# Whole VectorE passes, three steps moved to ScalarE, and tiles moved within 128 bytes in a two-block transformer kernel

## The chip, the cores and the metric

The kernel runs on one core of one Trainium2 chip. The metric is the device time of one execution in microseconds, as the median of several runs. Engines are called as the profile calls them: PE (TensorE), DVE (VectorE), ACT (ScalarE), POOL (GpSimd), SP (SyncE, which issues the loads).

## The reference

Two blocks run one after the other on x, 256 tokens of 2048 features, in fp32. Each block draws six modulation vectors from a conditioning vector c, mixes tokens in two ways, and ends with an FFN that has a causal convolution of width 3:

```python
mod = silu(c) @ w_ada + b_ada            # 2048 x 12288: six vectors of 2048
shift_m, scale_m, gate_m, shift_f, scale_f, gate_f = split(mod, 6)
h = rms_norm(x) * (1 + scale_m) + shift_m
proj = h @ w_in
# block 1: attention (8 heads of 128, own block, rel. bias) and an SSM (16 heads of 64, one chunk of 256)
#   p = softmax(logits);  attn = p @ v
#   y = (C B^T * exp(segsum(A))) @ (x * dt)
# block 2: a RWKV-7 scan (16 heads of 64) and window means (pool)
mix = concat(mixer_a, mixer_b) @ w_out
x = x + gate_m * mix
h = rms_norm(x) * (1 + scale_f) + shift_f
u = causal_dwconv3(h @ w_up)             # 2048 -> 2 x 5632
x = x + gate_f * ((silu(g) * val) @ w_down)   # g, val: the halves of u
```

A final rms_norm closes each block. Nearly all of the work is the products with w_in, w_out, w_up and w_down.

## The kernel before

**Products.** Tokens lie along the free axis (T = 256), so each matmul has a 128x128 weight tile as the stationary operand and 256 columns of x as the moving one, summed in a PSUM bank `acc`. An fp32 product is made of three float32r matmuls: weights and inputs are each split into a high part and a remainder, and `blk` issues hi·xh, hi·xl and lo·xh. A column of outputs (16 k-tiles, one 1 MB load into a tile `raw`) is worked off in two halves of 8 k-tiles. For each half ACT writes the high part `whi` in two pieces of 512 columns (`hi_steps`), DVE writes the remainder `wlo` = raw − whi in two pieces of 512 columns (`lo_steps`), and PE runs 24 matmuls. `raw` and `whi` and `wlo` have four buffers each, and the splitting runs two halves ahead of PE. The next load is issued by SP when the last half's `wlo` has been written (`issue`).

**The inputs** of a product are tiles [128, 512] whose first 256 columns are the high part and whose last 256 the remainder: h (tiles named `area`), the mixers' outputs (`mixa`, `mixb` in block 1, `mixA`, `mixB` in block 2), and the FFN's gated values, one tile `g` [128, 16, 512]. Where each lies within 128 bytes follows from the order in which the pools are filled: `whi`, `wlo` and `raw` at 64, the tiles of h at 0 in both FFNs, `mixa` and `mixb` at 96, `mixA` at 64, `g` at 96 in block 1 and at 64 in block 2, the tile `cb` at 96.

**Modulation.** A row of w_ada is a 1 MB load, mostly into a `raw` or a `mixb` tile that is not needed yet, in the FFNs into two tiles of their own (`far`). `ada` multiplies it with c (spread over the partitions in `cb`) on DVE and sums along the row, in two passes of 1024 columns that end in one column each of `mod` and `half`; each is followed by a read of DVE's accumulator, and `after` adds `half` to `mod`. Block 2 draws its late vectors (`adk`) in another way that is not touched.

**Attention and SSM** run as generators beside the products (one head, or one pair of heads, at a time). In attention the tile `L` holds logits, then probabilities; DVE normalises them with two `tensor_scalar` (128 and 256 columns) by `nm`, and copies the head's output out of PSUM to `at`, which lies in `mixa`. In the SSM a pair of heads has a tile `sg` [128, 768] with the decays (exp on ACT), which DVE multiplies with `G` (C·B^T) and with dt (`dtk`) in four `scalar_tensor_tensor`; `X` is a copy of the inputs out of PSUM by ACT.

**The order** on each engine is settled when the program is recorded: a clock model with a cost for each operation (`poll`) decides after each matmul block which generator's next step is put on its engine's queue. Every engine then works off its own queue in order. All instructions are recorded by one helper, line 302, so the profile's groups are told apart by the names of the tiles.

**The stages**, in us of the span: the first 16 columns of w_in with 32 modulation rows (0 to 165); the rest of w_in with attention and SSM (165 to 385); w_out of block 1 (385 to 515); its FFN (to 1269), three chunks of 32, 32 and 24 up columns (48 matmuls each) that each end with 16 down columns (48, 48 and 36 matmuls): up to 703, 974 and 1201 with the down columns of the first two from 703 to 793 and 974 to 1066; then block 2: w_in with the scan (1270 to 1640), w_out (1680 to 1762), and its FFN (1762 to 2508), with down columns from 1950 to 2041, 2215 to 2306 and 2437 to 2505. Between the FFN's up and down columns there is no break in PE's work.

Of the kernel before, what the change touches and what calls it, by code (L numbers as in the profile page):

```python
# [355 lines left out]
class K:  # L356
# [111 lines left out]
    def extra_steps(self, i, e):  # L468
# [6 lines left out]
        if e[0] == 'ada':  # L475
            return [lambda j=j: self.ada(e, j) for j in range(2)]
# [64 lines left out]
    def ada(self, e, j=0):  # L541
# [249 lines left out]
    def setup(self, ctx):  # L791
# [22 lines left out]
        self.half1 = self.pb1.tile([128, 96], F32, name='half1')  # L814
        self.half2 = c.tile([128, 96], F32, name='half2')
# [180 lines left out]
    def ffn_entries(self, blk, last_hook):  # L996
# [18 lines left out]
        for c, nk in enumerate(CH):  # L1015
            for j in range(j0, j0 + nk):
# [9 lines left out]
                def d2(acc, cv=cv, cg=cg, k=j - j0):  # L1026
                    y = yield from conv(acc, cv)
                    g = self.fg['g']
# [4 lines left out]
                    self.act(g[:, k, 0:T], y, AF.Identity)  # L1033
                    yield 'V'
                    self.nc.vector.tensor_sub(g[:, k, T:2 * T], y, g[:, k, 0:T].bitcast(F32))
                out.append(('w', self.full(A[f'wup{blk}'][2 * j], self.hrhs, d1)))
                out.append(('w', self.full(A[f'wup{blk}'][2 * j + 1], self.hrhs, d2)))
            for n in range(16):
# [7 lines left out]
                out.append(('w', self.full(A[f'wdn{blk}_{c}'][n], lambda k: self.fg['g'][:, k], d, nk)))  # L1046
# [5 lines left out]
    def wout_entries(self, blk, order, last_hook):  # L1052
        mod = self.mod1 if blk == 1 else self.mod2
        out = []
        for q, half in enumerate(order):
            for pr in range(8):
                ds = []
                for n in (2 * pr, 2 * pr + 1):
                    def d(acc, n=n, q=q):
                        assert (blk, 2) in self.ada_done  # L1060
                        yield from self.resid(acc, n, mod[:, 32 + n:33 + n])
                        if q == 1:
# [4 lines left out]
                                               lambda k: self.mix[k], ds)))  # L1067
# [27 lines left out]
    def attn_gen(self, h, box):  # L1095
# [36 lines left out]
        nc.vector.tensor_scalar(L[:, 0:128], L[:, 0:128], nm[:, 2:3], None, op0=MUL)  # L1132
        nc.vector.tensor_scalar(L[:, 128:384], L[:, 128:384], nm[:, 3:4], None, op0=MUL)
# [139 lines left out]
    def ssm_gen(self, i):  # L1273
# [11 lines left out]
        self.act(X, ps[:, 0:256], AF.Copy)  # L1285
# [872 lines left out]
```

## Time and profile before

| | |
|---|---|
| median of 3 runs | 2517.81 us (2504.33 to 2522.46) |
| profiled execution | 2520.43 us, span 2518.7 us, mean granted clock 0.978 |
| busy share of the span | PE 95%, DVE 81%, ACT 51%, POOL 3% |
| moved | 617.08 MB, mean 245 GB/s |
| chain that ended last | PE 74%, DVE 20%, issue 3%, ACT 2%, DMA 1% |

The span is the time from the first to the last instruction of the profiled execution; 1.7 us of its time lie around it. It is 2.6 us above the median. The shares are means over stages with different limits, so the table only says where to look: PE is busy nearly everywhere, DVE is next.

### The profile page before, as it was taken

What the parts mean: (1) busy time and instruction counts of PE and PEld (TensorE: products, weight loads), DVE (VectorE), ACT (ScalarE), POOL (GpSimd) and SP (SyncE); (2) the same over time, 40 slices, a digit from 0 to 9 for tenths busy, and PEclk for the clock granted to TensorE, in tenths of its full rate; (3) what the DMA queues carried; (4) which work ended last, traced back from release to release, by engine and by line L of the source; (5) the groups of instructions that cost most, each with busy time, mean ns of one, the idle gap of its engine ahead of it and who ended that gap; (6) DMA issues with size and microseconds to landing.
All of it is one profiled execution on the core that took longest, in us unless ns stands there. A gap on an engine that the chain in (4) does not pass through costs nothing.

```text
span 2518.7 us, 54091 instructions
## 1 busy us (share of the span) xinstructions
PE 2396.3 (95%) x22262; PEld 2323.6 (92%) x22262; DVE 2048.9 (81%) x4023; ACT 1280.0 (51%) x2515; POOL 80.3 (3%) x190
## 2 busy tenths in 40 slices
PE   6789898899999999999999999999999999999998
PEld 5779887899999999999988888889899999999998
DVE  6889999989878988787777999988898566755765
ACT  3236544455544554455566554434655455544554
POOL 0000000000000000000001222100000000000000
PEclk9899999899999999999999999989999999999999
DMA  9988787858787888785563444568687555555553
GB/s 347 347 319 316 269 300 286 314 207 315 290 311 287 304 299 301 288 297 197 190 210 126 160 168 170 201 235 301 234 310 274 185 184 199 187 198 184 188 178 123
DMA packets 93321, 617.08 MB, mean 245 GB/s; under 512 B 10473, under 2 KB 13809, under 8 KB 25233
## 3 DMA queue, kind: packets, MB, share of 16 engines
q1 hardware_dynamic: 89794, 604.93, 65.8%
q0 software_dynamic: 1984, 7.35, 0.8%
q8 instruction: 174, 2.85, 0.4%
q10 hardware_dynamic: 1296, 1.35, 0.2%
q14 instruction: 73, 0.60, 0.1%
HBM read 609.39 MB, written 4.21 MB: 244 GB/s over the span
## 4 chain that ended last, share of the span: by engine, by line
PE 74%; DVE 20%; issue 3%; ACT 2%; DMA 1%; ACTq 0%; DVEq 0%; SPq 0%
PE acc L302 68%; DVE wlo L302 4%; PE sB L302 4%; DVE raw L302 4%; DVE area L302 2%; DVE mixb L302 2%; ACT whi L302 1%; DVE t L302 1%; DVE adk L302 1%; PE sA L302 1%; DVE sg L302 1%; DVE slo L302 1%; DMA far<-wada 1%; DVE CK L302 0%; ACT area L302 0%
## 5 line engine op out<-in xcount | busy, mean ns | idle before, releaser
L302 PE MATMUL acc<-area,whi 128*128 128x256 f32 x8128 | 1474.9, 285 | 43.1 <-ACT area L302 39.5
L302 PEld LDWEIGHTS acc<-area,whi 128*128 128x128 f32 x8128 | 1260.3, 191 | 63.3 <-ACT area L302 45.3
L302 PE MATMUL acc<-area,wlo 128*128 128x256 f32 x3968 | 1113.2, 281 | 22.1 <-DVE wlo L302 21.8
L302 ACT ACTIVATE whi<-raw 128x512 fp32r<-128x512 f32 (+1 forms) x1472 | 834.8, 613 | 402.5 <-PE acc L302 309.4
L302 DVE TENSOR_TENSOR wlo<-raw,whi 128x512 fp32r<-128x512 f32 (+1 forms) x1472 | 930.2, 674 | 86.6 <-ACT whi L302 85.0
L302 PEld LDWEIGHTS acc<-area,wlo 128*128 128x128 f32 x3968 | 753.9, 190 | 25.3 <-DVE wlo L302 25.3
L302 PE MATMUL acc<-g,whi 128*128 128x256 f32 x2816 | 499.7, 281 | 0.0
L302 PEld LDWEIGHTS acc<-g,whi 128*128 128x128 f32 x2816 | 431.4, 188 | 0.0
L302 PE MATMUL acc<-g,wlo 128*128 128x256 f32 x1408 | 395.3, 281 | 0.0
L302 DVE SCALAR_TENSOR_TENSOR fy<-acc,vec,fy 128x255 f32<-128x255 f32 x352 | 169.1, 481 | 145.9 <-ACT fy L302 139.5
L302 PEld LDWEIGHTS acc<-g,wlo 128*128 128x128 f32 x1408 | 265.0, 188 | 0.0
L302 ACT ACTIVATE fy<-acc,vec 128x256 f32<-128x256 f32 x176 | 99.2, 565 | 262.3 <-PE acc L302 262.3
L302 DVE SCALAR_TENSOR_TENSOR far<-far,cb 128x1024 f32<-128x1024 f32 x160 | 191.2, 1218 | 11.8 <-DMA far<-wada 11.8
L302 DVE SCALAR_TENSOR_TENSOR area<-acc,mod,area 128x256 f32<-128x256 f32 x160 | 77.0, 481 | 102.1 <-PE acc L302 102.0
L302 DVE SCALAR_TENSOR_TENSOR raw<-raw,cb 128x1024 f32<-128x1024 f32 (+1 forms) x81 | 118.3, 1494 | 0.1
L302 ACT ACTIVATE area<-t,mod 128x256 fp32r<-128x256 f32 x64 | 32.2, 507 | 125.8 <-DVE t L302 125.8
L302 DVE SCALAR_TENSOR_TENSOR adk<-raw,vec,adk 128x512 f32<-128x512 f32 x120 | 91.0, 758 | 2.4
L302 DVE SCALAR_TENSOR_TENSOR mixb<-mixb,cb 128x1024 f32<-128x1024 f32 (+1 forms) x47 | 67.9, 1464 | 4.2 <-DMA mixb<-wada 4.2
L302 ACT ACTIVATE g<-fy 128x256 fp32r<-128x256 f32 x88 | 36.6, 416 | 67.3 <-DVE fy L302 67.3
L302 ACT ACT_TABLE_LOAD x48 | 61.6, 1283 | 12.1 <-DVE area L302 4.7
L302 ACT ACTIVATE t<-area 128x256 f32<-128x256 f32 x90 | 35.5, 411 | 61.2 <-DVE area L302 58.9
L302 ACT ACTIVATE fs<-fy 128x256 f32<-128x256 f32 x88 | 36.7, 417 | 47.7 <-DVE fy L302 46.0
(262 smaller groups left out, 1992.6 us busy)
## 6 DMA issues: line engine op xcount, KB each, us to landing
raw<-wup SPq DMA_DIRECT2D x176, 1024.0 KB, 6.3
far<-wada SPq DMA_DIRECT2D x80, 1024.0 KB, 4.9
raw<-win SPq DMA_DIRECT2D x64, 1024.0 KB, 5.5
raw<-wdn SPq DMA_DIRECT2D x64, 1024.0 KB, 5.2
raw<-wada SPq DMA_DIRECT2D x51, 1024.0 KB, 6.9
raw<-wout SPq DMA_DIRECT2D x32, 1024.0 KB, 5.5
raw<-wadk SPq DMA_DIRECT2D x32, 1024.0 KB, 6.1
mixb<-wada SPq DMA_DIRECT2D x29, 1024.0 KB, 7.5
```

The lines of the kernel that those rows point to most:

```text
L302: r = f(*a, **kw)
```

## The change

It has five parts.

1. `lo_steps`: the remainder of a half is written by one DVE instruction of 1024 columns, where there were two of 512. The next load is issued behind it.
2. `ada`: a row is multiplied and summed by one DVE instruction of 2048 columns, where there were two of 1024; `half1`, `half2` and the additions of them go.
3. Attention: the probabilities are normalised by two ACT instructions (scale from `nm`), and `at` is copied by ACT; both were DVE's.
4. SSM: dt is multiplied into `X` on ACT (four instructions of 64 columns in place of one copy of 256), and `sg` is multiplied with `G` in one DVE instruction of 768 columns, where there were four.
5. Placement: two unused tiles (64 and 96 bytes) move what lies behind them. `mixa` and `mixb` go from 96 to 0 within 128 bytes, `mixA` from 64 to 0, `cb` from 96 to 0. `g` goes to 0 in both blocks, and its 16 k-tiles lie in four groups of four, each 32 bytes further (0, 32, 64 and 96). What is read (`rhs`) is passed as a pair (high, remainder).

```diff
     def lo_steps(self, h):
-        def f(i, a, b):
-            if i == 0:
-                h.lo = self.spl.tile([128, 1024], F32R, name='wlo')
-            self.nc.vector.tensor_sub(h.lo[:, a:b], h.item.raw[:, h.off * 128 + a:h.off * 128 + b], h.hi[:, a:b].bitcast(F32))
-            if i == 1 and h is h.item.halves[-1]:
+        def f():
+            n = len(h.kts) * 128
+            h.lo = self.spl.tile([128, 1024], F32R, name='wlo')
+            self.nc.vector.tensor_sub(h.lo[:, 0:n], h.item.raw[:, h.off * 128:h.off * 128 + n], h.hi[:, 0:n].bitcast(F32))
+            if h is h.item.halves[-1]:
                 self.issue()
...
-        again = (lambda: self.far_back(raw)) if b.get('far') else self.issue
-        s = slice(j * 1024, j * 1024 + 1024)
-        self.stt(raw[:, s], raw[:, s], 1.0, self.cb[:, s], op0=MUL, op1=MUL, accum_out=b['acc'][j][:, col:col + 1])
-        if j == 0:
-            return
-        again()
+        self.stt(raw, raw, 1.0, self.cb, op0=MUL, op1=MUL, accum_out=b['acc'][:, col:col + 1])
+        if b.get('far'):
+            self.far_back(raw)
+        else:
+            self.issue()
...
+        self.tmp.tile([128, 16], F32, name='gap0', bufs=1)
         self.pb1 = self.open('b1', bufs=1)
+        self.pb1.tile([128, 24], F32, name='gap1')
...
+    def grhs(self, k):
+
+        g, o = self.fg['g'], k * 2 * T + self.fg['at'] + 8 * (k // 4)
+        return g[:, o:o + T], g[:, o + T:o + 2 * T]
...
-        nc.vector.tensor_scalar(L[:, 0:128], L[:, 0:128], nm[:, 2:3], None, op0=MUL)
-        nc.vector.tensor_scalar(L[:, 128:384], L[:, 128:384], nm[:, 3:4], None, op0=MUL)
+        yield 'A'
+        self.act(L[:, 0:128], L[:, 0:128], AF.Identity, scale=nm[:, 2:3])
+        self.act(L[:, 128:384], L[:, 128:384], AF.Identity, scale=nm[:, 3:4])
...
-        yield 'V'
-        nc.vector.tensor_copy(self.at[h].rearrange('p (a b) -> p a b', a=2), back(ps[:, 0:T]))
-        yield 'A'
+        yield 'A'
+        self.act(self.at[h].rearrange('p (a b) -> p a b', a=2), back(ps[:, 0:T]), AF.Copy)
...
-        self.act(X, ps[:, 0:256], AF.Copy)
+        for j in range(2):
+            for e in range(2):
+                hd = 16 * j + 2 * i + e
+                o = 128 * j + 64 * e
+                self.act(X[:, o:o + 64], ps[:, o:o + 64], AF.Identity, scale=self.dtk[:, hd:hd + 1])
...
-        for e in range(2):
-            o = e * 384
-            hd = 2 * i + e
-            self.stt(M[:, o:o + 256], G[:, 0:256], self.dtk[:, hd:hd + 1], sg[:, o:o + 256], op0=MUL, op1=MUL)
-            self.stt(M[:, o + 256:o + 384], G[:, 256:384], self.dtk[:, 16 + hd:17 + hd], sg[:, o + 256:o + 384], op0=MUL, op1=MUL)
+        M2 = M.rearrange('p (e c) -> p e c', e=2)
+        nc.vector.tensor_mul(M2, M2, G[:, None, :].to_broadcast([128, 2, 384]))
...
-        self.fg = {'p': p, 'g': p.tile([128, 16, 2 * T], F32R, name='g', bufs=1)}
+
+        self.fg = {'p': p, 'g': p.tile([128, 16 * 2 * T + 64], F32R, name='g', bufs=1), 'at': (0, 0)[blk - 1]}
```

What this does to the queues is seen in three places; the rows are the instructions in the order in which an engine works them off, with the tiles written and read. Numbers behind a name are those of its copies.

DVE in the rest of w_in, where attention runs: `area` rows are the convolution of the SSM's inputs, `RECIPROCAL nm` to `L` the end of one head's softmax. Before:

```order
L302 RECIPROCAL nm<-nm 128x2
L302 TENSOR_SCALAR L<-L,nm 128x128
L302 TENSOR_SCALAR L<-L,nm 128x256
L302 SCALAR_TENSOR_TENSOR area_94<-acc,vec_80,area_94 128x255
L302 SCALAR_TENSOR_TENSOR area_94<-acc,vec_80,area_94 128x254
L302 SCALAR_TENSOR_TENSOR area_94<-acc,vec_80,area_94 128x253
L302 SCALAR_TENSOR_TENSOR L<-sB,hd 128x256
L302 SCALAR_TENSOR_TENSOR L<-sB,hd 128x128
L302 TENSOR_REDUCE nm<-L 128x1 x2
L302 SCALAR_TENSOR_TENSOR mixb_112,mod_85<-mixb_112,cb 128x1024
L302 SCALAR_TENSOR_TENSOR mixb_112,half_87<-mixb_112,cb 128x1024
L302 TENSOR_TENSOR wlo<-raw,whi 128x512 x2
```

The same place after the change (`Adt` and `dtT` belong to the SSM's decays):

```order
L302 SCALAR_TENSOR_TENSOR L<-sB,hd 128x256
L302 SCALAR_TENSOR_TENSOR L<-sB,hd 128x128
L302 TENSOR_REDUCE nm<-L 128x1 x2
L302 TENSOR_TENSOR wlo<-raw,whi 128x1024
L302 RECIPROCAL nm<-nm 128x2
L302 SCALAR_TENSOR_TENSOR mixb_111,mod_87<-mixb_111,cb 128x2048
L302 TENSOR_SCALAR Adt<-dtT 16x256
L302 TENSOR_TENSOR wlo<-raw,whi 128x1024
```

The two rows on `L` behind the reciprocal have left DVE, the modulation row is one instruction, and so is each half's remainder.

DVE in w_out of block 1, where the SSM's heads run (`sg` from `sB` is a head's cumulated decay), before:

```order
L302 SCALAR_TENSOR_TENSOR mixb_112,mod_85<-mixb_112,cb 128x1024
L302 SCALAR_TENSOR_TENSOR mixb_112,half_87<-mixb_112,cb 128x1024
L302 TENSOR_TENSOR wlo<-raw,whi 128x512 x2
L302 SCALAR_TENSOR_TENSOR sg<-G_2607,dtk,sg 128x256
L302 SCALAR_TENSOR_TENSOR sg<-G_2607,dtk,sg 128x128
L302 SCALAR_TENSOR_TENSOR sg<-G_2607,dtk,sg 128x256
L302 SCALAR_TENSOR_TENSOR sg<-G_2607,dtk,sg 128x128
L302 TENSOR_TENSOR wlo<-raw,whi 128x512 x2
```

The same place after:

```order
L302 SCALAR_TENSOR_TENSOR sg<-sB,c_115 128x256
L302 SCALAR_TENSOR_TENSOR sg<-sB,c_115 128x128
L302 SCALAR_TENSOR_TENSOR sg<-sB,c_115 128x256
L302 SCALAR_TENSOR_TENSOR sg<-sB,c_115 128x128
L302 TENSOR_TENSOR sg<-sg,G_2557 128x768
L302 SCALAR_TENSOR_TENSOR raw,mod_87<-raw,cb 128x2048
L302 TENSOR_TENSOR wlo<-raw,whi 128x1024
L302 TENSOR_TENSOR sg<-sg,G_2557 128x768
```

The four products with `G` and `dtk` are one, and it follows the scans of its own pair closely.

ACT in the same stretch, where `X` is read out of PSUM, before:

```order
L302 ACTIVATE X<-sB 128x256
L302 ACTIVATE whi<-raw 128x512 x2
L302 ACTIVATE X<-sB 128x256
L302 ACTIVATE area_95<-acc 128x256
L302 ACTIVATE whi<-raw 128x512 x2
L302 ACTIVATE sg<-sg 128x768
L302 ACTIVATE whi<-raw 128x512
L302 ACTIVATE sg<-sg 128x768
```

And after:

```order
L302 ACTIVATE X<-sB,dtk 128x64 x4
L302 ACTIVATE whi<-raw 128x512 x3
L302 ACTIVATE X<-sB,dtk 128x64 x4
L302 ACTIVATE whi<-raw 128x512
L302 ACTIVATE area_94<-acc 128x256
L302 ACTIVATE whi<-raw 128x512
L302 ACT_TABLE_LOAD
L302 ACTIVATE sg<-sg 128x768
```

Each row of `X` has become four short ones, which stand between the same pieces of `whi`.

## Rows read from the trace of the kernel before

**Rows 1.** The page: busy time of each engine; the chain that ended last.
```profile
PE 2396.3 (95%) x22262; PEld 2323.6 (92%) x22262; DVE 2048.9 (81%) x4023; ACT 1280.0 (51%) x2515; POOL 80.3 (3%) x190
...
PE 74%; DVE 20%; issue 3%; ACT 2%; DMA 1%; ACTq 0%; DVEq 0%; SPq 0%
```

**Rows 2.** Busy time by stretch: stretch, length, engines (instructions), clock, DMA share, GB/s.
```profile
165.00:240.00 75.00, 71.70 (x591) 70.49 (x591) 65.38 (x140) 45.05 (x114) 0.00 (x0) 1.00 0.86 321
240.00:515.00 275.00, 241.90 (x1892) 230.75 (x1890) 267.34 (x547) 139.13 (x273) 0.00 (x0) 0.96 0.78 287
...
1330.00:1640.00 310.00, 302.14 (x5014) 264.87 (x5012) 281.91 (x701) 159.59 (x341) 70.02 (x163) 0.99 0.47 167
1680.00:1760.00 80.00, 78.55 (x650) 78.12 (x650) 74.23 (x135) 34.89 (x69) 0.00 (x0) 0.98 0.83 304
```

**Rows 3.** DVE groups, 240 to 515: operation, shape, count, busy us, mean ns, idle before.
```profile
L302 DVE TENSOR_TENSOR wlo<-raw,whi 128x512 fp32r<-128x512 f32 x144 | 94.0, 682 | 0.2
L302 DVE SCALAR_TENSOR_TENSOR raw<-raw,cb 128x1024 f32<-128x1024 f32 x50 | 58.8, 1217 | 0.1
L302 DVE SCALAR_TENSOR_TENSOR mixb<-mixb,cb 128x1024 f32<-128x1024 f32 x26 | 30.8, 1212 | 0.0
...
L302 DVE SCALAR_TENSOR_TENSOR sg<-G,dtk,sg 128x256 f32<-128x256 f32 x16 | 7.6, 476 | 0.0
...
L302 DVE SCALAR_TENSOR_TENSOR sg<-G,dtk,sg 128x128 f32<-128x128 f32 x16 | 5.5, 343 | 0.0
L302 DVE DVE_READ_ACCUMULATOR raw<-raw,cb 128x1 f32 x50 | 4.0, 81 | 0.0
...
L302 DVE TENSOR_TENSOR mixa<-t,mixa 128x256 fp32r<-128x256 f32 x8 | 3.0, 419 | 0.0
...
L302 DVE COPY mixa<-sB 128x256 f32<-128x256 f32 x3 | 1.2, 413 | 0.0
...
L302 DVE TENSOR_SCALAR L<-L,nm 128x256 f32<-128x256 f32 x2 | 0.7, 347 | 0.0
...
L302 DVE TENSOR_SCALAR L<-L,nm 128x128 f32<-128x128 f32 x2 | 0.6, 286 | 0.1
```

**Rows 4.** DVE groups of the start, 0 to 165 us: whole passes.
```profile
L302 DVE SCALAR_TENSOR_TENSOR raw<-raw,cb 128x2048 f32<-128x2048 f32 x21 | 47.6, 2287 | 0.0
...
L302 DVE TENSOR_TENSOR slo<-mixa,whi 128x1024 fp32r<-128x1024 f32 x16 | 19.6, 1225 | 6.9 <-ACT whi L302 6.9
```

**Rows 5.** ACT groups, 165 to 554 us.
```profile
L302 ACT ACTIVATE L<-L,nm 128x256 f32<-128x256 f32 x8 | 4.0, 497 | 0.0
...
L302 ACT ACTIVATE X<-sB 128x256 f32<-128x256 f32 x8 | 3.0, 376 | 11.8 <-PE sB L302 11.8
...
L302 ACT ACTIVATE mixa<-sB 128x256 f32<-128x256 f32 x5 | 1.9, 408 | 3.6 <-issue 3.6
```

**Rows 6.** PE's waits, 165 to 515 us: total us, times, longest.
```profile
PE acc L302 <- DVE wlo L302: 13.5, 10, 3.3
```

**Rows 7.** Busy time by stretch, both FFNs; PE's (x) counts matmuls.
```profile
600.00:690.00 90.00, 90.00 (x767) 90.00 (x766) 79.83 (x149) 49.82 (x97) 0.00 (x0) 1.00 0.81 300
710.00:790.00 80.00, 80.00 (x684) 80.00 (x684) 62.70 (x110) 32.60 (x57) 0.00 (x0) 1.00 0.80 304
800.00:960.00 160.00, 160.00 (x1361) 160.00 (x1360) 143.41 (x269) 88.54 (x171) 0.00 (x0) 1.00 0.79 291
...
1205.00:1265.00 60.00, 60.00 (x514) 60.00 (x513) 46.45 (x100) 37.27 (x89) 0.00 (x0) 1.00 0.58 199
1830.00:1940.00 110.00, 110.00 (x973) 110.00 (x972) 102.70 (x194) 62.77 (x122) 0.00 (x0) 1.00 0.80 299
1955.00:2035.00 80.00, 80.00 (x676) 80.00 (x675) 41.09 (x69) 32.33 (x56) 0.00 (x0) 1.00 0.54 190
2045.00:2205.00 160.00, 160.00 (x1414) 160.00 (x1414) 110.59 (x205) 92.36 (x176) 0.00 (x0) 1.00 0.55 194
```

**Rows 8.** The page's group of far modulation passes.
```profile
L302 DVE SCALAR_TENSOR_TENSOR far<-far,cb 128x1024 f32<-128x1024 f32 x160 | 191.2, 1218 | 11.8 <-DMA far<-wada 11.8
```

More of the change, by code (lines that the diff above doesn't have):

```diff
@@ L475, in extra_steps @@
         if e[0] == 'ada':
-            return [lambda j=j: self.ada(e, j) for j in range(2)]
+            return [lambda: self.ada(e)]
         return [lambda j=j: self.adk(e, j) for j in range(4)]
@@ L493, in lo_steps @@
     def lo_steps(self, h):
-        def f(i, a, b):
-            if i == 0:
-                h.lo = self.spl.tile([128, 1024], F32R, name='wlo')
-            self.nc.vector.tensor_sub(h.lo[:, a:b], h.item.raw[:, h.off * 128 + a:h.off * 128 + b], h.hi[:, a:b].bitcast(F32))
-            if i == 1 and h is h.item.halves[-1]:
+        def f():
[3 more added lines that the diff above has]
+            if h is h.item.halves[-1]:
                 self.issue()
-        return [lambda i=i, a=a, b=b: f(i, a, b) for i, (a, b) in enumerate(self.pieces(h))]
+        return [f]
     def issue(self):
@@ L596, in blk @@
         s = slice(i * 128, i * 128 + 128)
-        x = h.rhs(h.kts[i])
+        xh, xl = h.rhs(h.kts[i])
         st = h.start and i == 0
@@ L600, in blk @@
         acc = h.key['acc']
-        self.mm(acc, h.hi[:, s], x[:, 0:T], st, False)
-        self.mm(acc, h.hi[:, s], x[:, T:2 * T], False, False)
-        self.mm(acc, h.lo[:, s], x[:, 0:T], False, sp)
+        self.mm(acc, h.hi[:, s], xh, st, False)
+        self.mm(acc, h.hi[:, s], xl, False, False)
+        self.mm(acc, h.lo[:, s], xh, False, sp)
     LAT = 127.0
@@ L882, in ada_entries @@
                 src = self.a[f'wada{blk}'][n - 32 if (blk, g) == (2, 5) else n]
-                out.append(('ada', dict(src=src, acc=(mod, half), col=n, left=left, after=after, **kw)))
+                out.append(('ada', dict(src=src, acc=mod, col=n, left=left, after=after, **kw)))
         return out
@@ L983, in make_h, with two @@
         self.splits([(lambda k=k: f(k), self.hk(k), mod[:, g * 16 + k:g * 16 + k + 1]) for k in range(16)])
+    @staticmethod
+    def two(x):
+        return x[:, 0:T], x[:, T:2 * T]
     def hrhs(self, k):
-        return self.hk(k)
+        return self.two(self.hk(k))
+    def grhs(self, k):
+        g, o = self.fg['g'], k * 2 * T + self.fg['at'] + 8 * (k // 4)
+        return g[:, o:o + T], g[:, o + T:o + 2 * T]
     def resid(self, acc, n, gate):
@@ L1045, in d @@
                         last_hook(n)
-                out.append(('w', self.full(A[f'wdn{blk}_{c}'][n], lambda k: self.fg['g'][:, k], d, nk)))
+                out.append(('w', self.full(A[f'wdn{blk}_{c}'][n], self.grhs, d, nk)))
                 if n == 0:
@@ L1066, in wout_entries @@
                 out.append(('w', self.pairitem(self.a[f'wout{blk}'][half, pr], range(8 * half, 8 * half + 8),
-                                               lambda k: self.mix[k], ds)))
+                                               lambda k: self.two(self.mix[k]), ds)))
         return out
@@ L2094, in program @@
             for h in e[1].halves:
-                h.rhs = (lambda k: self.mixB[k - 8]) if i < 8 else (lambda k: self.mixA[k])
+                h.rhs = (lambda k: self.two(self.mixB[k - 8])) if i < 8 else (lambda k: self.two(self.mixA[k]))
         def out2():
```

14 lines of the change are left out of this document (4 added, 10 removed).

## Prediction

> **What bounds the kernel now.** I read the page's busy times and its chain first [rows 1]: PE is busy for 95% of the span and the chain runs over PE for 74% and over DVE for 20%. ACT is busy for half of the time. So a microsecond taken from DVE pays only where DVE, and not PE, ends last, and the next view must be the busy time by stretch [rows 2]. In the stretch 240 to 515 (the rest of w_in, then w_out of block 1) DVE is busy for 267.3 of 275.0 us, PE for 241.9: DVE bounds there. PE's waits agree, the longest sum being 13.5 us for `wlo` [rows 6]. From 165 to 240 it is PE (71.7 of 75.0 us, DVE 65.4). In block 2 PE is at 302.1 of 310.0 us in w_in and at 78.55 of 80.0 us in w_out: all that any engine could give back there is 7.9 and 1.45 us. In the FFNs PE is busy for 100% of every stretch that I looked at [rows 7], so only the length of a matmul counts. That makes two separate questions: how much of DVE's saving in 240 to 515 is realised, and whether the moved tiles alter a matmul's length.
>
> **Parts 1 to 4, DVE's work from 240 to 515.** Durations are from [rows 3], those of whole passes from [rows 4].
> - Remainders: 144 pieces are 72 halves. Two pieces take 2 x 682 = 1364 ns, one pass of 1024 columns 1225 ns in the start: 139 ns less, 10.0 us in all.
> - Modulation rows: 50 + 26 pieces are 38 rows. Each was 2 x 1215 + 2 x 81 = 2592 ns and becomes 2287 + 81 = 2368 ns: 224 ns less, 8.5 us.
> - Attention: the two normalisations, 2 x (347 + 286) ns, and three copies of 413 ns leave DVE: 2.5 us.
> - SSM: 16 x (476 + 343) ns = 13.1 us become eight products of 768 columns. No row has that size; it lies half way between 512 (682 ns) and 1024 (1225 ns), so about 0.95 us each, 7.6 us. That saves 5.5 us.
>
> Together 26.5 us of 267.3, which leaves DVE 240.8 us of work, just under PE's 241.9. So this part can't pay much more than DVE's saving: even if DVE took no time, PE's busy time allows 33 us. With two engines about equally loaded and a queue on each in fixed order, they wait for each other now and then; DVE kept PE waiting before while PE had 33 us to spare, afterwards both have about the same. I take 22 us, with bounds of 13 (half is lost to such waits) and 30 (PE's sums also go through faster, its granted clock having been 0.96 in this stretch [rows 2]). DMA is no end here: a share of 0.78 in 275 us is 215 us of full engines, and the stretch before it ran at 0.86.
>
> From 165 to 240 PE leaves 3.3 us idle: I take 2, bounds 0 and 3.3. In the first 165 us DVE's passes are whole already [rows 4]: 0.
>
> **ACT's added work.** Eight heads: normalising, near the 497 ns that an instruction with a per-partition operand takes on 256 columns [rows 5], so some 0.9 us for both, and a copy of 408 ns; eight pairs of heads: four short reads of PSUM in place of one of 376 ns; 64 columns instead of 256 leave at least the fixed part, and I put each at 0.3 us, between nothing and the 376 ns itself. That is 8 x 1.3 + 8 x (1.2 − 0.38) = 17 us over 350 us, in which ACT is busy for 45.1 + 139.1 = 184 us [rows 2]: it rises from 53% to 57%. The cover is this idle time, so I cost it at 0. If the cover were gone, because `whi` stands behind these steps on ACT's queue and DVE's remainder behind `whi`, a head's 1.3 us would have to outlast the two halves by which the splitting runs ahead, 48 matmuls of about 0.117 us or 5.6 us [rows 7].
>
> The Trainium skill speaks against this part: "ScalarE: Activation LUTs", Rules for kernel authors, wants a multiplication on VectorE, not on ScalarE. The row agrees as far as one instruction goes, since 256 columns take DVE 347 ns and ACT 497 ns. By that rule alone the attention would get slower by at most 8 x 2 x 0.15 us = 2.4 us; by the busy shares it costs nothing.
>
> **Block 2 before its FFN.** In w_in the two pieces of about 680 ns become one pass as above, a few us of DVE's 281.9, but PE is the bound: of its 7.9 idle us I take 2 (bounds 0 and 4). In w_out: 1 (0 and 1.45). The FFNs' entries, where h is made and little else runs, are not touched: 0 to 2, I take 1.
>
> **The FFNs, DVE's side.** DVE loses some 139 ns per half and 0.22 us in each of 80 far rows [rows 8]. None of it is seen while PE is busy for 100%: 0.
>
> **Part 5, the moved tiles.** The counts of [rows 7] give the length of a matmul: block 1's up columns 90/767 and 160/1361 = 117.4 and 117.6 ns, block 2's 110/973 and 160/1414 = 113.1 and 113.2 ns. It is the same instruction on tiles that lie alike within 128 bytes (h at 0, weights at 64). So one placement has two lengths, and placement doesn't settle it alone. What differs is what ran before: in block 1 the first up columns come after `mixb` at 96 and the later ones after `g` at 96, in block 2 after `mixA` and `g` at 64. The down columns took 117.0 ns (710 to 790) and 116.7 ns (1205 to 1265) with `g` at 96, and 118.3 ns with `g` at 64.
>
> The change doesn't touch h or the weights. With no mechanism in the rows that tells which length it takes, I leave block 1's up columns at 117.5 and block 2's at 113.1: 0. For the down columns `g` now lies at four places, two of which are those of before. There are 16 x (48 + 48 + 36) = 2112 of these matmuls in each block; I take 1 ns less in block 2 and nothing in block 1, and round down: −1.5 us. Bounds: both at 113.1 give −(3.8 + 5.2) x 2.112 = −19 us, both at 118.3 give +3 us.
>
> [...]
>
> **The sum.** −22 − 2 − 2 − 1 − 1 − 1.5 = −29.5, on the profiled execution's 2520.4 us: 2491. That execution was 2.6 us above the median of 2517.8, which I take off: **2488 us**. A measurement of this kernel can tell about 1% (25 us) from no change; the forecast lies just outside.
>
> **Rivals.**
> - *Block 2's up columns fall into the long rhythm.* Both later up stretches of block 1 that followed k-tiles of `g` at 96 ran at 117.6 ns, and the last group of four now lies at 96 in block 2 too, where `g` at 64 was followed by 113.2 ns. Against it: the first up columns of block 1 were long without any `g` ahead. Price: 32 + 24 columns of 48 matmuls = 2688 x 4.45 ns = 12 us: 2500 us. Chance 0.26.
> - *Block 1's up columns take the short rhythm.* They follow `mixb` and `g`, and both move; block 2 shows that h at 0 can run at 113.1 ns. Against it: nothing in h moved. All 88 columns: 4224 x 4.45 ns = 19 us less, 2469 us; only the later two chunks, 2476 us; the down columns in short rhythm too, some 2452 us. Chance 0.27, with 0.05 of it for the last.
> - *Slower: whole passes delay the remainders.* DVE works in order, and behind a far pass stand remainders and the reads of `acc` that set a bank free. A pass that was 1218 ns before the next instruction could start is 2287 now, 1.07 us more, 80 times [rows 8]: 86 us if all of it came through. It decides once a remainder is later than 5.6 us after its `whi`; if half came through, 43 us: 2531 us. For it: DVE is at 80/90 and 143/160 us in block 1's up columns. Against it: PE has no idle time there today, and the start runs with whole passes at full use of its loads. From about a third (29 us) the change is slower. Chance 0.06.
>
> The forecast, rhythms as they are, keeps 0.41.
>
> **How the numbers follow.** The forecast's own range is 2478 (30 of DVE's 33 us, and the upper bounds of block 2) to 2500 (13 in place of 22, and +3). With the rivals I give 2450 to 2515: below it lies the case in which all columns turn short, above it the slower rival and the long rhythm with little of DVE's saving. Faster by over 1% means under 2492.6: most of the forecast (0.28 of 0.41), nearly all of the short rhythm (0.26), a little of the long one (0.02), so 0.56. Slower by over 1% is most of the last rival: 0.04. Within 1%: 0.40.
>
> **What the profile of the changed kernel would show.** The end of w_out of block 1 some 24 us earlier, with DVE and PE about equally busy from 240 on; remainders of about 1.22 us, far rows of 2.29, products with `G` near 0.95; PE at 100% in the FFNs; 117.5 and 113.1 ns per matmul in the two up stretches, which is the step that I know least about. I would be wrong if w_out ended less than 13 us earlier (PE's waits then name `whi` or `raw`), or if either up stretch changed its rhythm.

## The result, and the profile after

The changed kernel takes 2491.81 us (median of 10 runs, 2485.70 to 2499.45), the kernel before in the same rounds 2505.64 us (10 runs, 2502.03 to 2522.46). The ratio is 0.9936, with a 95% interval of 0.9916 to 0.9957: 0.64% faster, about 14 us. The forecast was 2488 us from a base of 2518: the time is close, the gain is half of the forecast's 29.5 us. Two of the three runs on which the forecast stood, and the profiled execution, lay 12 to 17 us above the median of the ten.

The page of the changed kernel, busy time by engine, and the chain that ended last (compare [rows 1]):

```profile
PE 2368.0 (95%) x22262; PEld 2295.1 (92%) x22262; DVE 1993.7 (80%) x2975; ACT 1299.9 (52%) x2561; POOL 84.6 (3%) x188
...
PE 41%; DVE 5%; issue 2%; DMA 1%; ACT 1%; POOL 0%; DVEq 0%; SPq 0%; POOLq 0%; ACTq 0%
```

DVE's sum is 55 us smaller, ACT's 20 us larger. The shares of this chain add up to half of the span only (it was followed back no further), so they don't compare with the 20% of DVE before; the stages have to tell.

The profiled executions are 28 us apart (2518.7 and 2490.5 us of span). The first matmul of each stage, read from the timeline of PE, tells where:

| stage | before, us | after, us | difference |
|---|---|---|---|
| start and w_in of block 1, to 388.1 and 377.5 | 388.1 | 377.5 | −10.6 |
| w_out of block 1, to 517.5 and 508.6 | 129.4 | 131.1 | +1.7 |
| FFN of block 1, to 1276.2 and 1250.5 | 758.7 | 742.0 | −16.7 |
| w_in and w_out of block 2, to 1764.6 and 1738.1 | 488.4 | 487.5 | −0.9 |
| the rest | 754.1 | 752.4 | −1.7 |

So w_in of block 1 gave 10.6 us, w_out nothing, and more than half of the difference lies in block 1's FFN, where the forecast had put none. Both signs by which the forecast called itself wrong are there: w_out ends 8.9 us earlier, less than 13, and an up stretch changed its rhythm, as the rows of the FFNs show further down.

Busy time by stretch, the kernel before, cut where w_in ends (stretch, length, then PE, PEld, DVE, ACT, POOL with instructions, clock, DMA share, GB/s):

```profile
165.00:388.00 223.00, 205.71 (x1653) 197.40 (x1653) 212.31 (x441) 122.16 (x267) 0.00 (x0) 0.98 0.80 297
388.00:517.50 129.50, 108.62 (x832) 104.17 (x830) 121.52 (x250) 62.90 (x123) 0.00 (x0) 0.92 0.79 288
```

The same two stretches of the changed kernel:

```profile
165.00:377.50 212.50, 199.86 (x1642) 193.34 (x1642) 195.22 (x280) 133.72 (x309) 0.00 (x0) 0.99 0.83 309
377.50:508.60 131.10, 106.91 (x841) 102.43 (x839) 118.10 (x171) 62.25 (x130) 0.00 (x0) 0.94 0.78 288
```

DVE's work in both falls from 333.8 to 313.3 us, by 20.5, with 240 fewer instructions. Its idle time grows from 18.7 to 30.3 us, so 8.9 of the 20.5 us are seen as time. In w_in PE is now busy for 199.9 of 212.5 us.

DVE's groups of the changed kernel, 165 to 508 us (operation, shape, count, busy us, mean ns, idle before; compare [rows 3]):

```profile
L302 DVE TENSOR_TENSOR wlo<-raw,whi 128x1024 fp32r<-128x1024 f32 x93 | 112.4, 1219 | 3.8 <-ACT whi L302 3.8
L302 DVE SCALAR_TENSOR_TENSOR raw<-raw,cb 128x2048 f32<-128x2048 f32 x31 | 70.7, 2287 | 3.0 <-DMA raw<-wada 3.0
L302 DVE SCALAR_TENSOR_TENSOR mixb<-mixb,cb 128x2048 f32<-128x2048 f32 x18 | 41.2, 2287 | 3.6 <-DMA mixb<-wada 3.6
...
L302 DVE TENSOR_TENSOR sg<-sg,G 128x768 f32<-128x768 f32 x8 | 7.5, 963 | 0.0
```

Each instruction has the length that was forecast: 1219 ns, 2287 ns, 963 ns. Still DVE's busy time fell by only half of what their lengths gave (20.5 of some 38 us, worked out below).

The FFNs of the changed kernel, busy time by stretch; PE's (x) counts matmuls (compare [rows 7]):

```profile
600.00:690.00 90.00, 90.00 (x797) 90.00 (x796) 78.50 (x100) 52.56 (x100) 0.56 (x1) 1.00 0.86 320
710.00:790.00 80.00, 80.00 (x686) 80.00 (x686) 60.25 (x61) 33.72 (x60) 0.00 (x0) 1.00 0.79 295
800.00:950.00 150.00, 150.00 (x1326) 150.00 (x1325) 135.85 (x175) 86.31 (x166) 0.00 (x0) 1.00 0.85 310
...
1075.00:1190.00 115.00, 115.00 (x1012) 115.00 (x1011) 91.52 (x125) 66.22 (x133) 0.00 (x0) 1.00 0.65 229
1800.00:1910.00 110.00, 110.00 (x973) 110.00 (x972) 99.96 (x126) 64.13 (x123) 0.00 (x0) 1.00 0.82 299
1930.00:2005.00 75.00, 75.00 (x641) 75.00 (x640) 38.65 (x42) 31.12 (x54) 0.00 (x0) 1.00 0.55 195
2030.00:2180.00 150.00, 150.00 (x1326) 150.00 (x1325) 103.01 (x138) 87.34 (x165) 0.00 (x0) 1.00 0.56 197
```

Block 1's up columns are short now: 90/797 = 112.9, 150/1326 = 113.1 and 115/1012 = 113.6 ns per matmul, where they were 117.4 to 117.6. Block 2's are as before. The down columns take 116.6 (710 to 790) and 117.0 ns (1930 to 2005). A matmul that the edge of a stretch cuts is counted whole, so these quotients are off by up to half a nanosecond; from start to start in the timeline the two rhythms of the up columns are 113.3 and 117.8 ns.

### The profile page after: what moved, and what is told of

Its sections match the earlier page's. It is cut to its first block, busy times and chain, and to the rows that moved or that the text cites. A ratio compares the mean times of both kernels' runs of the same rounds, so it can differ in the third digit from the quotient of the medians.

```text
span 2490.5 us, 53198 instructions
## 1 busy us (share of the span) xinstructions
PE 2368.0 (95%) x22262; PEld 2295.1 (92%) x22262; DVE 1993.7 (80%) x2975; ACT 1299.9 (52%) x2561; POOL 84.6 (3%) x188
## 3 DMA queue, kind: packets, MB, share of 16 engines
q10 hardware_dynamic: 1296, 1.35, 0.2%
## 4 chain that ended last, share of the span: by engine, by line
PE 41%; DVE 5%; issue 2%; DMA 1%; ACT 1%; POOL 0%; DVEq 0%; SPq 0%; POOLq 0%; ACTq 0%
PE acc L302 37%; PE sB L302 4%; DVE adk L302 1%; DVE wlo L302 1%; PE sA L302 1%; DVE area L302 1%; DMA raw<-wadk 0%; DMA far<-wada 0%; DVE pad L302 0%; DVE CK L302 0%; DVE mixA L302 0%; DVE t L302 0%; ACT whi L302 0%; DVE y L302 0%; ACT area L302 0%
## 5 line engine op out<-in xcount | busy, mean ns | idle before, releaser
L302 PE MATMUL acc<-area,whi 128*128 128x256 f32 x8128 | 1454.0, 283 | 45.2 <-ACT area L302 41.4
L302 DVE TENSOR_TENSOR wlo<-raw,whi 128x1024 fp32r<-128x1024 f32 (+1 forms) x736 | 876.2, 1199 | 181.4 <-ACT whi L302 178.7
L302 DVE SCALAR_TENSOR_TENSOR far<-far,cb 128x2048 f32<-128x2048 f32 x80 | 182.6, 2283 | 10.6 <-DMA far<-wada 10.6
L302 DVE SCALAR_TENSOR_TENSOR raw<-raw,cb 128x2048 f32<-128x2048 f32 x51 | 116.0, 2287 | 3.0 <-DMA raw<-wada 3.0
L302 DVE SCALAR_TENSOR_TENSOR mixb<-mixb,cb 128x2048 f32<-128x2048 f32 x29 | 66.3, 2286 | 3.6 <-DMA mixb<-wada 3.6
L302 PE MATMUL acc<-mixa,whi 128*128 128x256 f32 x256 | 49.2, 294 | 12.1 <-DVE area L302 8.6
L302 PE MATMUL acc<-mixb,whi 128*128 128x256 f32 x256 | 48.1, 291 | 8.9 <-DVE area L302 4.6
```

The costliest lines, as they stand in the source:

```text
L302: r = f(*a, **kw)
```

## The experiments

**The two kernels once more (e1, e2).** One more profile of each, nothing edited.

> The kernel before, unchanged, profiled once more. Two theories about the 28 us between the two profiled executions, of which 18 us lie in block 1's FFN. Theory A (the length of a matmul in the FFNs' up columns varies from execution to execution, whatever the kernel): an execution near 2505 us has block 1's up columns, or some of its chunks, at 113 ns, one near 2520 us has them at 117.5 ns. Theory B (placement decides it): block 1's up columns are at 117.5 ns again whatever the time is, and the time is 2515 to 2522 us on the profile.

The kernel before took 2524.9 us. Its FFNs by stretch:

```profile
600.00:690.00 90.00, 90.00 (x767) 90.00 (x766) 79.86 (x150) 49.36 (x96) 0.00 (x0) 1.00 0.81 301
800.00:960.00 160.00, 160.00 (x1360) 160.00 (x1360) 141.14 (x264) 88.49 (x170) 0.00 (x0) 1.00 0.80 294
...
1830.00:1940.00 110.00, 110.00 (x973) 110.00 (x972) 103.36 (x196) 62.96 (x123) 0.00 (x0) 1.00 0.82 299
```

> The changed kernel, unchanged, profiled once more. Theory A: one of six up stretches may differ from the first profile; the time lies between 2486 and 2500 us and each 4.5 us of it goes with one third of a block's up columns. Theory B: all six up stretches at 113.3 ns again.

The changed kernel took 2486.97 us, all six up stretches short again (90/796 ns in the first).

What follows: an execution of the kernel before that takes 2525 us has block 1's up columns long in all the stretches shown, as both theories said (the time is above theory B's 2515 to 2522). That one near 2505 us has them short was not seen in a profile of this kernel; theory A stays open here. The 18 runs of the kernel before that were made beside e1 to e4 lay at 2501 to 2512 us (14) and at 2524 to 2529 us (4); the distance is about the 16.7 us of the FFN.

The timeline of PE shows when the length is settled. In all 13 profiles PE waits once for `wlo`, for 0.9 to 5.0 us, when it is 34 to 37 us into the up columns of a block. In e1 it does so in block 1 from 554.5 to 556.3 us; before and behind this wait:

```profile
532.00:554.00 22.00, 22.00 (x194) 21.93 (x193) 15.94 (x31) 16.66 (x32) 0.00 (x0) 1.00 0.64 229
560.00:700.00 140.00, 140.00 (x1191) 140.00 (x1191) 128.46 (x241) 77.35 (x149) 0.58 (x1) 1.00 0.83 308
```

The columns were short (22/194 = 113.4 ns) and are long behind it (140/1191 = 117.5 ns), with the same tiles and the same instructions. Across this wait the length changed in six of the 26 cases (two blocks in each of 13 profiles), to longer as to shorter, and never again before the block's first down column. So the length is settled when PE starts again after a wait, and it holds until the down columns come; what settles it is not shown.

**Parts 1 to 4 without part 5 (e3), and part 5 alone (e4).**

```diff
--- steps only: the changed kernel with
-        self.tmp.tile([128, 16], F32, name='gap0', bufs=1)
...
-        self.pb1.tile([128, 24], F32, name='gap1')
...
-        g, o = self.fg['g'], k * 2 * T + self.fg['at'] + 8 * (k // 4)
+        g, o = self.fg['g'], k * 2 * T + self.fg['at']
...
--- placement only: the kernel before with
...
+        self.tmp.tile([128, 16], F32, name='gap0', bufs=1)
...
+        self.pb1.tile([128, 24], F32, name='gap1')
...
+        g, o = self.fg['g'], k * 2 * T + self.fg['at'] + 8 * (k // 4)
...
```

> Parts 1 to 4 with the old placement (mixa, mixb at 96, mixA and g as before, g not in groups). Theory A: most of the 14 us is here, 9 to 12 us under the kernel before, and w_out of block 1 ends near 508 us in the profile. Theory B: 3 to 9 us under it at most, since block 1's up columns stay at 117.5 ns.

2488.67 us (7 runs, 2484.46 to 2496.31), ratio 0.9914 (0.9882 to 0.9946): 18.6 us under the median beside it, more than either theory gave. w_in ends at 377.4, w_out at 507.2 us. Block 1's up columns are short in its profile (90/796 ns), with h, weights, `mixa`, `mixb` and `g` where they lay before.

> Part 5 alone (the two gaps, g in four groups), DVE's and ACT's work as before. Theory A: 0 to 5 us under the kernel before (the down columns and w_out in the new places), and the end of w_out at 515 us as before. Theory B: 8 us or more under it, with all up columns at 113.3 ns.

2507.62 us (12 runs, 2500.02 to 2515.43), ratio 0.9984 (0.9961 to 1.0008): no difference that the interval, −10 to +2 us, can tell. w_in ends at 387.5 and w_out at 517.5 us, as before. Its FFNs:

```profile
600.00:690.00 90.00, 90.00 (x797) 90.00 (x796) 84.12 (x159) 51.08 (x100) 0.57 (x1) 1.00 0.84 308
...
1830.00:1930.00 100.00, 100.00 (x852) 100.00 (x851) 90.06 (x171) 54.70 (x107) 0.00 (x0) 1.00 0.77 285
2045.00:2195.00 150.00, 150.00 (x1326) 150.00 (x1325) 104.11 (x193) 87.32 (x166) 0.00 (x0) 1.00 0.56 197
```

Block 1 ran short (112.9 ns), and the first up stretch of block 2 ran long (100/852 = 117.4), the next one short (113.1), with the same tiles in the same places. Theory B falls: the gain is in parts 1 to 4. The length of an up column's matmul is not settled by where its tiles lie.

**Whole passes alone (e5), ACT's steps alone (e6).** The kernel before with parts 1 and 2, and with parts 3 and 4.

```diff
--- whole passes only
-        return [lambda i=i, a=a, b=b: f(i, a, b) for i, (a, b) in enumerate(self.pieces(h))]
+        return [f]
...
+        self.stt(raw, raw, 1.0, self.cb, op0=MUL, op1=MUL, accum_out=b['acc'][:, col:col + 1])
--- ACT's steps only
...
+        self.act(L[:, 0:128], L[:, 0:128], AF.Identity, scale=nm[:, 2:3])
...
+        nc.vector.tensor_mul(M2, M2, G[:, None, :].to_broadcast([128, 2, 384]))
```

> Parts 1 and 2 alone (whole passes for the remainders and the modulation rows), old placement, attention and SSM as before. In the profile of parts 1 to 4 the rest of w_in is 10.6 us shorter and w_out of block 1 is not. Theory D (DVE's busy time is the bound, so each microsecond taken from it counts alike): about half of the 10.6 us is here, 15.7 of DVE's 29.6 us being these passes: the rest of w_in ends 5 to 6 us earlier than before's 388. Theory P (what counts is who holds a bank or a buffer, not the sum): 0 to 3 us, or a loss in w_out.

2498.11 us (10 runs), ratio 0.9937 (0.9906 to 0.9967). w_in and w_out by stretch:

```profile
165.00:381.80 216.80, 201.28 (x1653) 193.51 (x1653) 206.00 (x321) 122.05 (x268) 0.00 (x0) 1.00 0.82 304
381.80:510.60 128.80, 105.84 (x830) 100.90 (x828) 117.61 (x178) 60.86 (x122) 0.00 (x0) 0.94 0.79 292
```

> Parts 3 and 4 alone (the steps on ACT, one product with G), passes of 512 and 1024 as before, old placement. Theory D: the other half, the rest of w_in ends 4 to 6 us earlier (attention's 8.3 us of DVE lie there), and w_out 2 to 4 us shorter (5.6 us of the SSM's). Theory P: w_in 6 to 10 us earlier, w_out the same.

2510.78 us (10 runs), ratio 0.9989 (0.9952 to 1.0026). Its profiled execution had block 1's up columns long (90/767 ns). w_in and w_out:

```profile
165.00:380.40 215.40, 199.03 (x1629) 192.15 (x1629) 199.65 (x396) 131.31 (x306) 0.00 (x0) 0.99 0.82 303
380.40:511.90 131.50, 111.16 (x840) 106.47 (x838) 123.65 (x246) 64.33 (x131) 0.00 (x0) 0.91 0.79 290
```

DVE's work adds up: 333.8 us before, 323.6 with the whole passes (−10.2), 323.3 with ACT's steps (−10.5), 313.0 with both. The time doesn't: up to the FFN 352.5 us before, 345.6, 346.9, and 342.2 with both; 6.9 and 5.6 us alone, 10.3 together. Nearly all of it is in w_in (6.2 and 7.6 us), as theory P had it for ACT's steps; the size of the whole passes' share is theory D's. The whole times say something else: by them the whole passes alone have all of the gain (0.9937) and ACT's steps none (0.9989). Five of e6's ten runs lie at 2515 to 2526 us and the other five at 2500 to 2506, with no such split in e5 (2491 to 2504), so these ratios mix the stages' savings with the rhythm of the FFN, and the stages are the better measure of the parts.

**What bounds w_out.** The changed kernel, with the 48 modulation rows of 165 to 508 us summed by half (e7), loaded by half (e8), or both (e11). Half of these sums is left out, so the result is not the reference's.

```diff
--- half the sum
-        self.stt(raw, raw, 1.0, self.cb, op0=MUL, op1=MUL, accum_out=b['acc'][:, col:col + 1])
+        n = 1024 if b['mid'] else 2048
+        self.stt(raw[:, 0:n], raw[:, 0:n], 1.0, self.cb[:, 0:n], op0=MUL, op1=MUL, accum_out=b['acc'][:, col:col + 1])
...
--- half the load (and two passes over that half)
-                self.nc.sync.dma_start(t, e[1]['src'])
+                n = 1024 if e[1].get('mid') else 2048
+                self.nc.sync.dma_start(t[:, 0:n], e[1]['src'][:, 0:n])
...
```

> The changed kernel, but the 48 modulation rows between 165 and 508 us are multiplied and summed over their first 1024 columns only (the other half of these sums is left out); the loads stay whole. Theory D: w_out of block 1 (131 us, 18 rows) gets 15 to 19 us shorter, the rest of w_in 10 us or more. Theory L (the loads are the bound: four raw slots, each given back and loaded again in turn): w_out at most 6 us shorter.

```profile
165.00:368.30 203.30, 198.11 (x1641) 193.33 (x1640) 169.81 (x292) 137.52 (x321) 0.00 (x0) 0.99 0.86 320
368.30:480.90 112.60, 103.11 (x831) 99.02 (x829) 94.47 (x159) 55.50 (x116) 0.00 (x0) 0.95 0.89 340
```

> The changed kernel, but the same 48 modulation rows are loaded by half (512 KB), and DVE makes two passes over that half (so these sums are wrong by the half that is left out, and DVE works 0.2 us more for each row). Theory D: w_out of block 1 stays at 128 to 135 us. Theory L: w_out gets 10 us shorter or more, since 9 of its 35 MB are gone.

```profile
165.00:386.00 221.00, 205.89 (x1666) 197.87 (x1665) 205.57 (x350) 137.31 (x320) 0.00 (x0) 0.98 0.66 224
386.00:509.80 123.80, 104.62 (x825) 100.78 (x824) 115.06 (x197) 58.65 (x118) 0.00 (x0) 0.94 0.67 236
```

> The changed kernel with the 48 modulation rows between 165 and 508 us loaded by half and summed by half (the other half of these sums is left out). With the sums alone halved, w_out of block 1 took 112.6 us instead of 131, with the loads alone halved 123.9. Theory D (DVE bounds it, loads stand behind): 105 to 113 us, no more than the two together. Theory L: 100 us or less.

```profile
366.00:477.00 111.00, 101.52 (x831) 98.69 (x829) 96.97 (x165) 60.52 (x120) 0.00 (x0) 0.97 0.76 273
```

With half the sums w_out takes 112.6 us, 18.5 less, with DVE's work 23.6 us smaller (118.1 to 94.5): most of it comes through. w_in gives 9.2 us for 25.4 us less of DVE's work (195.2 to 169.8). In the changed kernel PE's waits for `wlo` in w_in were 9.1 us; in e7 none is left, and PE is busy for 198.1 of 203.3 us: there PE has become the bound.

Half the loads give w_out 7.3 us, which neither theory had (128 to 135 us, or 121 and less), and cost w_in 8.5, where the second pass makes DVE's work 10.4 us larger. Part of this is one modulation row that moved: w_out holds 18 of them in the changed kernel and 17 in e7, e8 and e11. Over both stages together, where that doesn't count, half the sums give 27.7 us (343.6 to 315.9), half the loads cost 1.2 (344.8, with 7.3 us more work on DVE), and half the loads beside half the sums give 3.9 (312.0; w_in ends at 366.0). So DVE bounds w_out, as theory D said; theory L falls, and the loads are worth a few microseconds at most.

**Where g lies, again.** The kernel before with `g` of block 1 at 64 (e9); the changed kernel with `g` at 96 in both blocks and not in groups (e10).

```diff
--- the kernel before
...
+        self.fg = {'p': p, 'g': p.tile([128, 16 * 2 * T + 64], F32R, name='g', bufs=1), 'at': (24, 0)[blk - 1]}
--- the changed kernel
-        g, o = self.fg['g'], k * 2 * T + self.fg['at'] + 8 * (k // 4)
+        g, o = self.fg['g'], k * 2 * T + self.fg['at']
...
-        self.fg = {'p': p, 'g': p.tile([128, 16 * 2 * T + 64], F32R, name='g', bufs=1), 'at': (0, 0)[blk - 1]}
+        self.fg = {'p': p, 'g': p.tile([128, 16 * 2 * T + 64], F32R, name='g', bufs=1), 'at': (24, 24)[blk - 1]}
```

> The kernel before with g of block 1 moved from 96 to 64 within 128 bytes (24 floats further in a tile padded by 256 bytes), nothing else. The runs of the kernel before fall into two groups, most at 2501 to 2513 us and about three in ten at 2523 to 2533. Theory R (the length of a matmul is drawn anew when PE starts again at a block's up columns; h's columns keep it; g at 96 hands it on to the next up columns, g at 64 or in groups lets them start short): the upper group is gone, a long start now costs 32 x 48 matmuls x 4.45 ns = 7 us instead of 19, so all runs lie at 2500 to 2517. Theory S (the length follows from what ran before, not from g): about three in ten still at 2520 or more.

2511.06 us (9 runs, 2508.63 to 2518.70), ratio 1.0034 (1.0022 to 1.0047): 0.34% slower, 7.3 us. Its first up, down and second up stretch:

```profile
600.00:690.00 90.00, 90.00 (x766) 90.00 (x765) 79.85 (x150) 49.77 (x96) 0.00 (x0) 1.00 0.82 299
720.00:780.00 60.00, 60.00 (x502) 60.00 (x502) 44.48 (x77) 23.88 (x42) 0.00 (x0) 1.00 0.78 288
820.00:940.00 120.00, 120.00 (x1061) 120.00 (x1060) 111.19 (x210) 68.52 (x134) 0.00 (x0) 1.00 0.86 315
```

The up columns start long (90/766 = 117.5 ns) and are short after `g` at 64 (120/1061 = 113.1), as theory R said; in the profiles of before with `g` at 96 they stayed long. That the upper group of runs vanishes says nothing, since none of the 14 runs of the kernel before beside it was in that group either. (e1 to e4 ran on one chip, e5 to e8 on a second, e9 to e11 on a third, and of the kernel before 4 of 18, 6 of 19 and 0 of 14 runs were in that group; whether it goes with the chip is open.) What is slower is the down columns: 60/502 = 119.5 ns, against 117.0 and 116.7 with `g` at 96 in [rows 7]. For 2112 of them that is 5 to 6 of the 7.3 us.

> The changed kernel with g at 96 in both blocks and not in groups. Theory R: each block that starts long stays long through all its up columns, 19 us each, so that some runs lie at 2505 us or above (block 2 started long in 3 of 9 profiles so far, block 1 in 3 of 9 and never with whole passes); in the profile either all three up stretches of a block are at 117.5 ns or none is. Theory S: the runs spread as the changed kernel's did, 2486 to 2500.

2487.62 us (6 runs, 2481.37 to 2491.49), ratio 0.9934 (0.9919 to 0.9948). The first up, down and second up stretch of block 2:

```profile
1790.00:1900.00 110.00, 110.00 (x936) 110.00 (x935) 96.08 (x123) 61.92 (x118) 0.00 (x0) 1.00 0.83 304
1935.00:2005.00 70.00, 70.00 (x602) 70.00 (x601) 37.31 (x39) 28.85 (x51) 0.00 (x0) 1.00 0.56 195
2030.00:2180.00 150.00, 150.00 (x1326) 150.00 (x1325) 103.00 (x137) 87.27 (x165) 0.00 (x0) 1.00 0.56 197
```

A long start (110/936 = 117.5 ns) with `g` at 96 behind it (70/602 = 116.3), and the next up columns short (113.1). Here theory R falls: `g` at 96 doesn't always hand the long rhythm on. The changed kernel with `g` at one place is as fast as with four (0.9934 and 0.9936).

## Why the prediction was right and wrong

**The number came close by luck.** The forecast took 29.5 us off a base of 2518. The base was 12 us too high (2505.64 in the end), and the gain 16 us too large (13.8). Within the profiles two errors of about the same size stand against each other: w_in and w_out gave 8.9 us instead of 24, and block 1's FFN 16.7 instead of 0.

**Right: DVE was the bound from 240 to 515, and its saving is where the stages got shorter.** Parts 1 to 4 alone give the whole gain (0.9914), part 5 none that can be told (0.9984). With DVE's sums halved w_out gets shorter by nearly as much as DVE is relieved of.

**Wrong: the step "the cost of two pieces against one pass".** The forecast took 2 x 682 against 1225 ns, 139 ns a half, and 224 ns a modulation row. The lengths were right, but an instruction's length is not what it costs on a queue: the next one starts before it ends. The forecast's own row had the sign of it: 144 pieces of 682 ns are 98.2 us, and DVE was busy with them for 94.0 [rows 3]. DVE's timeline, before (start us, length us, engine, instruction):

```profile
413.31 1.26 DVE L302 TENSOR_TENSOR wlo<-raw,whi 128x512 fp32r<-128x512 f32 x2
414.50 0.47 DVE L302 SCALAR_TENSOR_TENSOR area<-acc,mod,area 128x256 f32<-128x256 f32 x1
414.89 1.21 DVE L302 SCALAR_TENSOR_TENSOR mixb<-mixb,cb 128x1024 f32<-128x1024 f32 x1
416.03 0.08 DVE L302 DVE_READ_ACCUMULATOR mixb<-mixb,cb 128x1 f32 x1
416.03 1.22 DVE L302 SCALAR_TENSOR_TENSOR mixb<-mixb,cb 128x1024 f32<-128x1024 f32 x1
417.18 0.08 DVE L302 DVE_READ_ACCUMULATOR mixb<-mixb,cb 128x1 f32 x1
417.18 0.68 DVE L302 TENSOR_TENSOR wlo<-raw,whi 128x512 fp32r<-128x512 f32 x1
```

From the first remainder's start to the next instruction's it is 414.50 − 413.31 = 1.19 us for two pieces, and from 414.89 to 417.18 = 2.29 us for a modulation row in two, with both reads of the accumulator lying under the pass that follows. The changed kernel:

```profile
439.31 2.29 DVE L302 SCALAR_TENSOR_TENSOR raw<-raw,cb 128x2048 f32<-128x2048 f32 x1
441.52 0.08 DVE L302 DVE_READ_ACCUMULATOR raw<-raw,cb 128x1 f32 x1
441.52 1.22 DVE L302 TENSOR_TENSOR wlo<-raw,whi 128x1024 fp32r<-128x1024 f32 x1
442.66 0.48 DVE L302 SCALAR_TENSOR_TENSOR area<-acc,mod,area 128x256 f32<-128x256 f32 x1
```

One modulation pass takes 441.52 − 439.31 = 2.21 us, one remainder 442.66 − 441.52 = 1.14 us. Over all instructions from 165 us to the end of w_out that the next one follows without a pause, the median from start to start is 602 ns for a remainder of 512 columns and 1136 for one of 1024, 1145 ns for a modulation piece of 1024 and 2210 for one of 2048. Each is about 0.08 us less than the length. The savings are 0.07 us a half and 0.08 us a row; for 93 halves and 48 rows that is 10.2 us, and e5 shows 10.2. By lengths it was 13 + 11 = 24 us for the same count. The same overlap makes ACT's steps worth 10.5 us of DVE's time instead of 14. This is the term that was mis-sized: 38 us by lengths over 165 to 515, 20.5 measured.

**Wrong: how much of it comes through, 24 us forecast for w_in and w_out, and ACT's added work at no cost.** 8.9 us of the 20.5 came through, 10.3 in e3; the other 11.6 became idle time of DVE. The forecast looked for this loss between DVE and PE. The rows show it between DVE and ACT. DVE's waits, before (165 to 517.5 us), and in the changed kernel (165 to 508):

```profile
DVE ssuma L302 <- ACT t L302: 2.2, 3, 1.5
...
DVE ssuma L302 <- ACT t L302: 8.5, 10, 1.8
DVE wlo L302 <- ACT whi L302: 3.8, 5, 1.3
```

(`ssuma` sums the squares `t` that ACT makes.) All of DVE's waits for ACT up to the FFN add up to 6.1 us before and 15.1 in the changed kernel, so that 9 of the 11.6 us are of this kind. The other profiles agree: 6.6 to 7.1 us with neither change (e1, e4, e9), 9.3 with the whole passes alone (e5), 10.1 with ACT's steps alone (e6), 14.5 to 15.6 with both (e2, e3, e10). In w_in they go with ACT's steps: 4.0 to 5.8 us in the five profiles without them, 8.8 to 10.6 in the five with them. So the cover was not whole. ACT's added steps have the lengths that were forecast, 391 and 496 ns for normalising and 316 ns for the short reads of PSUM (ACT's groups, 165 to 546 us):

```profile
L302 ACT ACTIVATE L<-L,nm 128x256 f32<-128x256 f32 x16 | 7.9, 496 | 0.0
...
L302 ACT ACTIVATE X<-sB,dtk 128x64 f32<-128x64 f32 x32 | 7.3, 316 | 6.8 <-PE sB L302 6.8
...
L302 ACT ACTIVATE L<-L,nm 128x128 f32<-128x128 f32 x16 | 6.3, 391 | 0.9 <-DVE nm L302 0.9
```

What ACT's mean busy share (57%) didn't tell is that DVE would wait for single results behind them. That these steps delay `t` and `whi` on ACT's queue is the likely reason; no run takes them apart.

In w_out the two passes save 34 x 0.07 + 18 x 0.08 = 3.8 us. DVE's work there fell by 3.4 us and its idle time grew by 5.0; a shorter w_in leaves one row and half a half more to it (33.5 halves and 17 rows before, 34 halves and 18 rows now). Repeats of w_out differ by 1 to 3 us (129.4 and 132.5 us in the two profiles of before, 131.1 and 130.4 in the two of the changed kernel), so its +1.7 us is no change. PE's waits of the changed kernel, 165 to 508 us, answer to [rows 6]:

```profile
PE acc L302 <- DVE area L302: 13.2, 6, 4.6
PE acc L302 <- DVE wlo L302: 9.3, 10, 1.6
```

The forecast had named `whi` or `raw` for this case; these are the largest instead. The wait for remainders fell from 13.5 to 9.3 us. The one for `area`, the sum that frees a bank, rose from 10.8 to 13.2 us, with one of 4.6 us (478.8 to 483.4) in which two whole passes stand ahead of it on DVE's queue, the second of them waiting 1.35 us for its load. That is the mechanism of the slower rival, in one place; it did not decide.

**The base.** The forecast subtracted 29.5 us from an execution whose first FFN ran in long rhythm. Like for like the stages other than that FFN differ by 11.5 us between the two profiles, and the medians by 13.8. The short-rhythm rival (0.27) is what the two profiled executions show, 16.7 us for its price of 19, and it is no effect of placement, which it gave as its reason: with the old placement it came too (e3, e5), with the new one a block started long (e4). In the profiles with whole passes (after, e2, e3, e5, e7, e8, e10, e11) block 1 always ran short, in those with the old passes it ran long in four of five (before, e1, e6, and e9 in its first chunk). The runs go the same way: none of the 33 runs of after, e3, e5 and e10 lies in an upper group, while the kernel before and e6 have one. So the rhythm goes with the whole passes, which also move the wait for `wlo` that settles it; that they are its cause is not shown.

**The long rhythm's rival in block 2** came in part, in e4, e6, e7 and e10: its first up columns ran long, 5 to 6 us, never the later ones. What decides the rhythm when PE starts again stays open. Tried were the places of `g` (0 to 96 in groups, 64, 96) and of `mixa`, `mixb` and `mixA` (e3, e4); none fixes it.

**Block 2 and the entries.** Forecast 4 us together; w_in and w_out of block 2 gave 0.9 us in the first profile and 4.3 in e2. The down columns: forecast −1.5 us; in block 2 they take 117.0 instead of 118.3 ns, −2.7 us for 2112, in block 1 116.6 instead of 117.0. For them the place of `g` does count: block 2's took 118.3 ns with `g` at 64 (before), 117.0 in the four groups (after) and 116.3 at 96 (e10). Block 1 had 96 already; there e3, with `g` at 96 and a short rhythm, took 80/691 = 115.8 ns, so that the groups cost it nearly 2 us.

## What to carry to other kernels

Cost an instruction on a busy queue from its start to the next one's start in the timeline, not by its length: joining two passes of 512 columns saved 0.07 us here, not 0.14. A count times the length that is larger than the group's busy time is the sign of it. Then look, result by result, at what the relieved engine waits for next: here 9 of 20.5 us came back as waits for the engine that had taken over the work, although that one was busy for little more than half of the time. And before a forecast is hung on one profile, look whether a repeated instruction has two lengths in it: one execution's rhythm was worth more here (16.7 us) than the rest of the change (11.5).

## What the runs showed that was not expected

- The same matmul of 256 columns on tiles in the same places takes 113.1 or 117.5 ns for hundreds of microseconds on end, at a granted clock of 1.00 in both (rows of the FFNs above). The length changed across a wait of PE (e1), and at the change between up and down columns also without one (e9, e10).
- A read of DVE's accumulator costs the queue next to nothing: it starts together with the pass behind it (416.03 and 441.52 us), and a pass of 1024 columns with a read behind it takes 1145 ns from start to start, one without 1136.
- Two savings on one engine's queue add in its busy time to 0.3 us (10.2 + 10.5 against 20.8 us in e3) and don't in time (6.9 + 5.6 against 10.3).
